# Transposes for attention and for the first branch: TensorE's, or VectorE's blocks by way of DRAM

## The chip, the cores and the metric

One core of a Trainium2 chip runs the kernel. The metric is the time of one execution on the device, in microseconds; each kernel is run several times and the median is given. Everything is float32.

## The reference

One layer of a hybrid network on 512 tokens of width 1024. It has two feed-forward halves and, between them, a mixing stage with two branches: a gated mLSTM and a forgetting attention of 16 heads of 64. All modulations (shift, scale, gate) come from one vector c through `w_ada`.

```python
u = rms_norm(x, ffn1_norm_g) * (1 + sc1) + sh1
x = x + 0.5 * g1 * swiglu(u, ffn1_w_in, ffn1_w_out)

u = rms_norm(x, mix_norm_g) * (1 + sc2) + sh2
z = u @ w_mix + b_mix            # q_m,k_m,v_m,o_m,i_m,f_m, q_f,k_f,v_f,f_f, g_a,g_b
h_m = mlstm_chunkwise(q_m, k_m, v_m, i_m, f_m)               # 4 heads, 128 / 256 wide
y_a = sigmoid(o_m) * rms_norm(h_m, mlstm_norm_g)             # first branch
y_b = forgetting_attention(q_f, k_f, v_f, f_f, fox_q_norm_g, fox_k_norm_g)  # 16 heads of 64
merged = sigmoid(g_a) * (y_a @ w_branch_a) + sigmoid(g_b) * (y_b @ w_branch_b)
x = x + g2 * (merged @ w_out)

u = rms_norm(x, ffn2_norm_g) * (1 + sc3) + sh3
x = x + 0.5 * g3 * swiglu(u, ffn2_w_in, ffn2_w_out)
```

## The kernel before

Every float32 product is made of three matmuls on split operands (`mm3`, lines 125 to 129): high by high, low by high, high by low. A weight comes from DRAM into one of three buffers `raw` (L92), ScalarE writes its high half `wh` (L102), VectorE its low half `wl` (L104), four buffers each. The same three `raw` buffers serve the rows of `w_ada`, which VectorE accumulates into `acc` (L302, L304); those are drawn in small steps (`self.ada`) wherever the program calls for one. All loads and stores named here are issued by SyncE (SP), in one queue.

The program is written as a dataflow: tiles come from pools with a fixed number of buffers, a scheduler orders the instructions of each engine, and waits follow from the tiles' reads and writes. So an edit in one place can change the order on every engine, near it and further away.

The mixing stage goes like this. `mlstm_h` (L1081) makes h of one mLSTM head in four blocks of 128 tokens (tile `hn`), scales each token's row (L1106, VectorE) and stores it to DRAM, `h_d` (L1107). `fox_qkv` (L1110) makes q and k of a group of four attention heads with tokens on the partitions (tiles `tk`, four of 128x512, normalized at L1138). `fox_t` (L1175) turns q and k of one pair of heads so that the 64 features of each head are on the partitions: TensorE transposes 128x128 blocks against an identity into PSUM (L1193), and ScalarE (L1198, L1202) and VectorE (L1200) split the result into high and low halves `fq`, `fk`, `klz`. `fox_s` (L1205) makes a head's scores and their softmax S, `fox_p` (L1235) transposes S (L1250) and splits it into `Ph` (L1248) and `Pl` (L1249), and `fox_o` (L1266) makes the output (L1280, then yt at L1283 and yb at L1284).

Between these steps, which wait much for each other, the main loop puts GEMM work: `advance(fill, n)` takes n steps of a generator. For the first twelve heads the filler is `fox_qkv` of the next group and then `gate` (one GEMM of 24 matmuls into PSUM tile g, a tanh at L1324, a store of `tg` to `g_d` at L1326); for the last four it is `y_a` (L1287) for m = 0 to 7. One `y_a` multiplies a 128-column slice of `w_mix` (w, 24 matmuls), takes the tanh `th` (L1300), loads a 128-column slice of h from DRAM (tile `ht`, L1302), transposes it on TensorE (L1305), scales it on ScalarE into `ya` (L1307), and multiplies with the gate (L1308). From m = 4 on each also draws two steps of `self.ada`. After it, two more gates and the branch's GEMMs follow, with `split_y` (L1343) in front of them.

The tiles `tk` and `ht` come from the same pool entry `"tok"` with four buffers. PSUM tiles come from `gbank` (GEMMs, g) and `tbank` (all else, t).

Of the kernel before, what the change touches and what calls it, by code (L numbers as in the profile page):

```python
# [11 lines left out]
F32 = mybir.dt.float32  # L12
F32R = mybir.dt.float32r
I32 = mybir.dt.int32
AF = mybir.ActivationFunctionType
# [5 lines left out]
P = 128  # L21
T = 512
NT = 4
D = 1024
NK = 8
# [19 lines left out]
MUL, ADD, SUB, MAX, MIN = ALU.mult, ALU.add, ALU.subtract, ALU.max, ALU.min  # L45


class Layer:
    def __init__(self, tc, es, A, out, dbg=None):
        self.tc, self.nc, self.es, self.A, self.out = tc, tc.nc, es, A, out  # L50
        self.dbg = dbg or {}
        pool = lambda name, **k: es.enter_context(tc.tile_pool(name=name, **k))
        self.cp = pool("const", bufs=1)
        self.up = pool("u", bufs=1)
        self.xp = pool("x", bufs=1)
        self.wp = pool("w", bufs=4)
        self.sp = pool("small", bufs=4)
        self.pg = pool("pg", bufs=4, space=PSUM)
        self.pt = pool("pt", bufs=4, space=PSUM)
        self.dp = pool("scr", bufs=1, space=DRAM)  # L60
        self.lo_after = None
        self.n = self.nx = self.now = 0
        self.due = []
        self.free = self.pin = lambda i: i

    def nm(self, s):
# [7 lines left out]
    def tick(self, n=1):  # L74
        for _ in range(n):
            self.now += 1
            for f in [f for t, f in self.due if t == self.now]:
                f()

    def tmp(self, pool, name):  # L80

# [999 lines left out]
    def mlstm_h(self, h, ip):  # L1081
        nc, sp = self.nc, self.sp
        (Wh, Wl), (vh, vl) = self.W[h], self.vt[h]
        ss = sp.tile([P, NT], F32, name=self.nm("hs"), tag="hs", bufs=2)
        hs = []
        for tb in range(NT):
            if tb % 2 == 0:
                h2 = ip.tile([P, 2, 256], F32, name=self.nm("hn"), tag="bc", bufs=4)
            ps = self.tbank()
# [12 lines left out]
        v = sp.tile([P, NT], F32, name=self.nm("hv"), tag="hv", bufs=2)  # L1102
        nc.vector.tensor_scalar(v, ss, 1.0 / 256, EPS, op0=MUL, op1=ADD)
        r = self.rsqrt(v, NT)
        for tb in range(NT):
            nc.vector.tensor_scalar(hs[tb], hs[tb], r[:, tb:tb + 1], None, op0=MUL)  # L1106
            nc.sync.dma_start(self.h_d[tb * P:(tb + 1) * P, h * 256:(h + 1) * 256], hs[tb])  # L1107


    def fox_qkv(self, g, ip):  # L1110

        nc, sp, w = self.nc, self.sp, self.A["w_mix"][0]
        o = g * 256
        bb = self.bias_bcast([(QF + o, 256), (KF + o, 256)], ip)
        tok = [ip.tile([P, 512], F32, name=self.nm("tk"), tag="tok", bufs=4) for _ in range(NT)]
# [20 lines left out]
        for tb in range(NT):  # L1136
            t3 = tok[tb].rearrange("p (h d) -> p h d", h=8)
            nc.vector.tensor_tensor(t3, t3, r[:, tb * 8:(tb + 1) * 8].unsqueeze(2).to_broadcast([P, 8, 64]), op=MUL)  # L1138
        if g == 3:
            self.fx[g] = tok, self.fx[g]  # L1140
            return
        gs = ((0,), (1,), (2, 3))[g]
        n = len(gs) * 256
# [12 lines left out]
        def mkv(ch):  # L1156
# [5 lines left out]
                wh, wl = self.split(r, sh)  # L1162
                return wh, wl, k * ch, k
            return make
        self.fx[g] = (tok, vts[0])
        if len(gs) > 1:
            self.fx[3] = vts[1]
# [7 lines left out]
    def fox_t(self, p, ap):  # L1175
# [11 lines left out]
        new = lambda n: ap.tile([P, T], F32R, name=self.nm(n), tag="qk", bufs=16)  # L1187
        q, k, kl = [new("fq") for _ in range(2)], [new("fk") for _ in range(2)], self.klz[p % 2]
        for i, R in ((0, R_FQ), (1, R_FK)):
            c = i * 256 + pr * P  # L1190
            b = self.tbank()
            for tb in range(NT):
                nc.tensor.transpose(b[:, tb * P:(tb + 1) * P], tok[tb][:, c:c + P], self.ident)  # L1193
            gc = self.colA[:, R + p:R + p + 1]
            for h in range(2):
                own, oth = lohi[h], lohi[1 - h]
                d = (q, k)[i][h]
                nc.scalar.activation(d[own, :], b[own, :], AF.Copy, scale=gc[own, :])  # L1198
                lo = q[h][oth, :] if i == 0 else kl[h][own, :]
                nc.vector.scalar_tensor_tensor(lo, b[own, :], gc[own, :], d[own, :], op0=MUL, op1=SUB)  # L1200
                if i:
                    nc.scalar.activation(k[h][oth, :], b[own, :], AF.Copy, scale=gc[own, :])  # L1202
# [81 lines left out]
        nc.vector.tensor_tensor(self.yb[2 * g + pr][rows, :], po[rows, :], tmp[rows, :], op=ADD)  # L1284


    def y_a(self, m, ap, ip):  # L1287
        nc = self.nc
        def step():
            if m >= NK // 2:  # L1290
                self.tick()
                next(self.ada)
        ps = self.gbank()
        w = self.w_stat(self.A["w_mix"][0], OM + m * P)
        self.gemm_stat(ps, w, 0, T, range(0, 4))
        step()
        yield
        self.gemm_stat(ps, w, 0, T, range(4, 8))
        th = self.tmp(ip, "th")
        nc.scalar.activation(th, ps, AF.Tanh, scale=0.5, bias=self.hom[:, m:m + 1])  # L1300
        ht = ip.tile([P, NT, P], F32, name=self.nm("ht"), tag="tok", bufs=4)
        nc.sync.dma_start(ht, self.h_d[:, m * P:(m + 1) * P].rearrange("(b p) n -> p b n", p=P))  # L1302
        b = self.tbank()
        for tb in range(NT):
            nc.tensor.transpose(b[:, tb * P:(tb + 1) * P], ht[:, tb, :], self.ident)  # L1305
        ya = ap.tile([P, T], F32, name=self.nm("ya"), tag="qk", bufs=16)
        nc.scalar.activation(ya, b, AF.Copy, scale=self.hmg[:, m:m + 1])  # L1307
# [46 lines left out]
    def run(self):  # L1354
# [2 lines left out]
        self.x_d = self.dp.tile([T, D], F32, name="x_d")  # L1357
        self.h_d = self.dp.tile([T, D], F32, name="h_d")
        self.v0_d = [self.dp.tile([P, 256], F32, name=f"v0_d{tb}") for tb in range(NT)]
        self.g_d = [self.dp.tile([P, T], F32, name=f"g_d{i}") for i in range(2 * NK)]  # L1360

        self.ntmp, self.xn_tiles, self.gb_tag = 4, self.xn_ffn, ("gb", 2)
# [144 lines left out]
        with tc.tile_pool(name="att", bufs=1) as ip:  # L1507
# [18 lines left out]
            def advance(gen, n):  # L1526
                for _ in range(n):
                    next(gen, None)
# [130 lines left out]
```

## Time and profile before

| | |
|---|---|
| median of 3 runs | 1320.24 us (1319.11 to 1320.57) |
| profiled execution, its own time | 1320.06 us |
| its span in the trace | 1318.2 us |
| TensorE clock granted | 1.000 |
| mLSTM heads and group 0 of q and k | 480 to about 550 us |
| attention loop | about 550 to 810 us |
| `y_a` GEMMs, m = 0 to 7 | about 753 to 819 us |

In the rows of the trace, PE is TensorE's matmuls, DVE VectorE, ACT ScalarE, SP SyncE. A row of the timeline has the start in us, the duration, the engine, the line of the kernel, the operation, output<-inputs by the program's names, and how many instructions are put together. A matmul's duration includes the pipeline's filling, so two matmuls of 0.39 us that start 0.23 us apart overlap; what one costs TensorE is read from the starts. The text in square brackets is the idle time ahead of an instruction and what ended it.

### The profile page before, as it was taken

Reading aid. Unit: us, or ns where it says so; the run is one execution under the profiler, and the core shown is the slowest. Engines: PE = TensorE matmul, PEld = TensorE weight load, DVE = VectorE, ACT = ScalarE, POOL = GpSimd, SP = SyncE. Lnnn points to the kernel's source line nnn. Section 1 sums busy time; section 2 is a strip of 40 time slices with the busy share of each in tenths; the row PEclk is TensorE's granted clock in tenths of the full one; section 3 lists DMA queues with packets and bytes.
Section 4 is the critical chain, followed back from the end, with each engine's and each line's share of the span. In section 5 each row is a group of like instructions: output and inputs, shape, how many; then the busy total and the mean of one; then the engine's idle time right before and its main releaser. Section 6 shows DMA issues by size and latency. Waiting matters only on the chain.

```text
span 1318.2 us, 17786 instructions
## 1 busy us (share of the span) xinstructions
PE 1303.2 (99%) x6341; PEld 1092.7 (83%) x6341; DVE 955.4 (72%) x1736; ACT 629.6 (48%) x1054; POOL 36.9 (3%) x57
## 2 busy tenths in 40 slices
PE   7999999999999999999999999999999999999998
PEld 6788888888899888888888888888898888888887
DVE  6887767478688687887887778777567556635787
ACT  5533232355476555566666666334372223223651
POOL 1000000000010101000000000003000000000000
PEclk9999999999999999999999999999999999999999
DMA  9899978465845334533342536777539777634574
GB/s 294 262 326 303 320 268 281 136 193 163 301 126 145 106 111 129 160 104 109 88 129 73 167 105 190 219 251 237 184 104 327 248 238 279 219 100 136 171 263 149
DMA packets 204488, 254.18 MB, mean 193 GB/s; under 512 B 15008, under 2 KB 146752, under 8 KB 204400
## 3 DMA queue, kind: packets, MB, share of 16 engines
q1 hardware_dynamic: 204016, 252.98, 60.4%
q8 instruction: 50, 0.82, 0.3%
q14 instruction: 38, 0.31, 0.1%
q0 software_dynamic: 320, 0.06, 0.0%
q10 hardware_dynamic: 64, 0.02, 0.0%
HBM read 217.28 MB, written 35.72 MB: 192 GB/s over the span
## 4 chain that ended last, share of the span: by engine, by line
PE 93%; DVE 3%; ACT 2%; DMA 1%; issue 1%; ACTq 0%; DVEq 0%
PE g L129 23%; PE g L127 23%; PE g L128 23%; PE t L127 4%; PE t L129 4%; PE t L128 4%; PE g L897 2%; PE t L1280 1%; PE t L1250 1%; PE t L1221 1%; PE t L897 1%; PE t L1222 1%; PE t L797 1%; ACT uh L263 0%; DVE wl L104 0%
## 5 line engine op out<-in xcount | busy, mean ns | idle before, releaser
L102 ACT ACTIVATE wh<-raw 128x1024 fp32r<-128x1024 f32 (+2 forms) x246 | 249.3, 1017 | 373.6 <-PE g L128 128.7
L104 DVE TENSOR_TENSOR wl<-raw,wh 128x1024 fp32r<-128x1024 f32 (+2 forms) x246 | 287.6, 1172 | 160.1 <-ACT wh L102 135.6
L127 PE MATMUL g<-uh,wh 128*128 128x512 f32 (+1 forms) x880 | 341.0, 388 | 0.0
L128 PE MATMUL g<-ul,wh 128*128 128x512 f32 (+1 forms) x880 | 339.5, 386 | 0.4 <-DVE ul L268 0.4
L129 PE MATMUL g<-uh,wl 128*128 128x512 f32 (+1 forms) x880 | 339.6, 386 | 0.0
L129 PEld LDWEIGHTS g<-uh,wl 128*128 128x128 f32 x880 | 165.3, 188 | 33.6
L128 PEld LDWEIGHTS g<-ul,wh 128*128 128x128 f32 x880 | 165.4, 188 | 33.0 <-DVE ul L268 0.6
L127 PEld LDWEIGHTS g<-uh,wh 128*128 128x128 f32 x880 | 165.3, 188 | 32.8 <-issue 0.6
L304 DVE SCALAR_TENSOR_TENSOR acc<-raw,ccol,acc 128x512 f32<-128x512 f32 (+1 forms) x70 | 66.7, 974 | 42.8 <-DMA raw<-in_w_ada_dram 42.7
L127 PE MATMUL g<-wh,uh 128*128 128x512 f32 (+1 forms) x256 | 97.5, 381 | 0.0
L129 PE MATMUL g<-wh,ul 128*128 128x512 f32 (+1 forms) x256 | 96.7, 378 | 0.0
L128 PE MATMUL g<-wl,uh 128*128 128x512 f32 (+1 forms) x256 | 96.4, 377 | 0.0
L127 PE MATMUL t<-wh,A 128*128 128x512 f32 x176 | 68.6, 390 | 0.0
L128 PE MATMUL t<-wl,A 128*128 128x512 f32 x176 | 68.5, 389 | 0.0
L129 PEld LDWEIGHTS g<-wh,ul 128*128 128x128 f32 x256 | 48.2, 188 | 9.0
L127 PEld LDWEIGHTS g<-wh,uh 128*128 128x128 f32 x256 | 48.2, 188 | 8.7 <-DVE tk L1118 0.5
L128 PEld LDWEIGHTS g<-wl,uh 128*128 128x128 f32 x256 | 48.2, 188 | 8.3
L129 PE MATMUL g<-yh,wl 128*128 128x512 f32 x128 | 50.0, 391 | 0.1
L127 PE MATMUL g<-yh,wh 128*128 128x512 f32 x128 | 49.8, 389 | 0.0
L128 PE MATMUL g<-yl,wh 128*128 128x512 f32 x128 | 49.8, 389 | 0.0
L420 ACT ACTIVATE A<-E 128x768 fp32r<-128x768 f32 x22 | 18.6, 846 | 53.4 <-DVE E L419 53.4
L1232 ACT ACTIVATE S<-S,mn 128x128 f32<-128x128 f32 (+1 forms) x64 | 35.5, 556 | 16.1 <-DVE mn L1224 9.9
(353 smaller groups left out, 2242.1 us busy)
## 6 DMA issues: line engine op xcount, KB each, us to landing
raw<-in_ffn_w_in_dram SPq DMA_DIRECT2D x82, 512.0 KB, 4.9
raw<-in_w_ada_dram SPq DMA_DIRECT2D x56, 512.0 KB, 5.7
raw<-in_w_mix_dram SPq DMA_DIRECT2D x46, 512.0 KB, 4.2
sa<-in_ffn_w_out_dram SPq DMA_DIRECT2D x22, 512.0 KB, 5.5
sb<-in_ffn_w_out_dram SPq DMA_DIRECT2D x44, 256.0 KB, 5.2
ws<-sa SPq DMA_DIRECT2D x22, 512.0 KB, 4.6
ws<-sb SPq DMA_DIRECT2D x44, 256.0 KB, 5.0
raw<-ws SPq DMA_DIRECT2D x44, 256.0 KB, 3.5
```

The costliest lines, as they stand in the source:

```text
L102: nc.scalar.activation(hi, src, AF.Copy)
L104: self.last_lo = nc.vector.tensor_tensor(lo, src, hi, op=SUB)
L127: pin(mm(ps, lh, rh, start=start, stop=False))
L128: pin(mm(ps, lh, rl, start=False, stop=False))
L129: self.last_mm = pin(mm(ps, ll, rh, start=False, stop=stop))
L304: nc.vector.scalar_tensor_tensor(a, r[:, s], c, a, op0=MUL, op1=ADD)
L420: nc.scalar.activation(A1[:, 0:3, :], E[:, 0:3, :], AF.Copy)
L797: pin(nc.tensor.transpose(cb[:, 384:512], self.ident, self.ident))
L897: pin(nc.tensor.matmul(acc_ps[b], (wl if p == 1 else wh)[:, b % 2, s], self.ul[k] if p == 2 else self.uh[k], start=k == 0 and p == 0, stop ...
L1221: nc.tensor.matmul(ps[:, :w], q[:, s], k[:, :w], start=True, stop=False)
L1222: nc.tensor.matmul(ps[:, :w], q[:, s], kl[:, :w], start=False, stop=True)
L1232: nc.scalar.activation(S[:, ws], S[:, ws], AF.Exp, scale=-1.0, bias=m, accum_out=sm[:, qb:qb + 1])
```

## The change

Three things are done in another way.

1. `mlstm_h`: the rows of h are scaled by ScalarE. Two blocks of 128 tokens by 256 make a tile of 128x512; VectorE transposes it in place in squares of 32x32, and one store instead of two takes it to `h_d`, one step of the filler later.
2. `fox_qkv` for groups 1 to 3: after L1138 VectorE transposes each `tk` tile in the same way, in place; it is stored to a new DRAM array `t_d[g]` one step later, and three steps later `bring` loads four tiles `fT` of 128x512 from it, in the order 0, 2, 1, 3 (q and k of the first pair of heads, then of the second). Each tile takes four loads (`blocks`) of 32 partitions by 16 squares by 32 elements, that is 512 runs of 128 bytes, so that the squares land transposed as a whole. `fox_t` then splits from `fT` in SBUF; group 0 stays with TensorE.
3. `y_a`: `ht` is loaded by `blocks` too, one m ahead (two at m = 0), and ScalarE scales it straight from SBUF. 

The delays are kept by a list `self.posts`, which `advance` counts down. In the new order of instructions the lines have other numbers: L1131 is a load of `blocks`, L1167 the store of `tk`, L105 the load of raw, L115 and L117 wh and wl, L1348 is th, L1350 ya, L1285 Ph, L1320 yt, L1369 the gate's store, L140 to L142 the three matmuls.

```diff
+    def post(self, steps, f):
+        self.posts.append([steps, f])
+
+    def advance(self, gen, n):
+        for _ in range(n):
+            next(gen, None)
+            for p in self.posts[:]:
+                p[0] -= 1
+                if p[0] < 0:
+                    self.posts.remove(p)
+                    p[1]()
...
         for tb in range(NT):
-            nc.vector.tensor_scalar(hs[tb], hs[tb], r[:, tb:tb + 1], None, op0=MUL)
-            nc.sync.dma_start(self.h_d[tb * P:(tb + 1) * P, h * 256:(h + 1) * 256], hs[tb])
+            nc.scalar.activation(hs[tb], hs[tb], AF.Copy, scale=r[:, tb:tb + 1])
+            if tb % 2:
+                t = h2s[tb // 2].rearrange("p b n -> p (b n)")
+                nc.vector.transpose(t, t)
+                self.post(1, lambda t=t, b=tb - 1: nc.sync.dma_start(
+                    self.h_d[b * P:(b + 2) * P, h * 256:(h + 1) * 256].rearrange("(b p) n -> p b n", p=P),
+                    t.rearrange("p (b n) -> p b n", b=2)))
+
+    def blocks(self, t, src):
+
+        for j in range(4):
+            self.nc.sync.dma_start(t[32 * j:32 * j + 32, :].rearrange("a (t b) -> a t b", b=32),
+                                   src[:, 32 * j:32 * j + 32].rearrange("(t a) b -> a t b", a=32))
...
             nc.vector.tensor_tensor(t3, t3, r[:, tb * 8:(tb + 1) * 8].unsqueeze(2).to_broadcast([P, 8, 64]), op=MUL)
+            if g:
+                t = tok[tb]
+                nc.vector.transpose(t, t)
+                self.post(1, lambda t=t, tb=tb: nc.sync.dma_start(self.t_d[g][tb * P:(tb + 1) * P, :], t))
+        def bring():
+            qk = [ip.tile([P, T], F32, name=self.nm("fT"), tag="tok", bufs=4) for _ in range(4)]
+            for n in (0, 2, 1, 3):
+                self.blocks(qk[n], self.t_d[g][:, n * P:(n + 1) * P])
+            self.fx[g][0] = qk
+        if g:
+            self.post(3, bring)
...
-            b = self.tbank()
-            for tb in range(NT):
-                nc.tensor.transpose(b[:, tb * P:(tb + 1) * P], tok[tb][:, c:c + P], self.ident)
+            if g:
+                b = tok[2 * i + pr]
+            else:
+                b = self.tbank()
+                c = i * 256 + pr * P
+                for tb in range(NT):
+                    nc.tensor.transpose(b[:, tb * P:(tb + 1) * P], tok[tb][:, c:c + P], self.ident)
...
+    def ht_load(self, m, ip):
+        t = ip.tile([P, T], F32, name=self.nm("ht"), tag="tok", bufs=4)
+        self.blocks(t, self.h_d[:, m * P:(m + 1) * P])
+        self.ht.append(t)
+
     def y_a(self, m, ap, ip):
...
         w = self.w_stat(self.A["w_mix"][0], OM + m * P)
+        if m == 0:
+            self.ht = []
+            self.ht_load(0, ip)
         self.gemm_stat(ps, w, 0, T, range(0, 4))
         step()
         yield
+        if m + 1 < NK:
+            self.ht_load(m + 1, ip)
         self.gemm_stat(ps, w, 0, T, range(4, 8))
+        ht = self.ht[m]
         th = self.tmp(ip, "th")
         nc.scalar.activation(th, ps, AF.Tanh, scale=0.5, bias=self.hom[:, m:m + 1])
-        ht = ip.tile([P, NT, P], F32, name=self.nm("ht"), tag="tok", bufs=4)
-        nc.sync.dma_start(ht, self.h_d[:, m * P:(m + 1) * P].rearrange("(b p) n -> p b n", p=P))
-        b = self.tbank()
-        for tb in range(NT):
-            nc.tensor.transpose(b[:, tb * P:(tb + 1) * P], ht[:, tb, :], self.ident)
         ya = ap.tile([P, T], F32, name=self.nm("ya"), tag="qk", bufs=16)
-        nc.scalar.activation(ya, b, AF.Copy, scale=self.hmg[:, m:m + 1])
+        nc.scalar.activation(ya, ht, AF.Copy, scale=self.hmg[:, m:m + 1])
```

Three places in the order of instructions follow; the numbers behind the names are the program's own, and they differ between the two kernels.

SyncE before, at the start of `y_a`: raw_7572, raw_7673 and raw_7756 are the weights of m = 2, 3 and 4.

```order
L92 DMA raw_7572<-in_w_mix_dram 128x8x128
L1326 DMA g_d_96<-tg_7150 128x512
L92 DMA raw_7673<-in_w_mix_dram 128x8x128
L1210 DMA A_1425_7505<-A_d 128x512
L1326 DMA g_d_97<-tg_7214 128x512
L92 DMA raw_7756<-in_w_mix_dram 128x8x128
L1326 DMA g_d_98<-tg_7260 128x512
L1302 DMA ht_7448<-h_d 128x4x128
```

SyncE now, at the same place: raw_7518, raw_7601 and raw_7700 are the weights of m = 1, 2 and 3, tg_7308 and tg_7398 those of the last two gates ahead of m = 0.

```order
L1369 DMA g_d_102<-tg_7308 128x512
L1131 DMA ht_7438<-h_d 32x16x32
L1369 DMA g_d_103<-tg_7398 128x512
L1131 DMA ht_7438<-h_d 32x16x32 x3
L1131 DMA ht_7467<-h_d 32x16x32 x4
L105 DMA raw_7518<-in_w_mix_dram 128x8x128
L1247 DMA A_1425_7536<-A_d 128x512
L1131 DMA ht_7566<-h_d 32x16x32 x4
L105 DMA raw_7601<-in_w_mix_dram 128x8x128
L1131 DMA ht_7647<-h_d 32x16x32 x4
```

Before, the weights of m = 2 to 4 stood ahead of the first load of h; now the weight of m = 1 stands behind the last gate's store and behind the eight loads of the first two tiles of h, and each later weight behind four more.

ScalarE before, around the last three `y_a`: th_7913 and th_8004 are the tanh of m = 5 and 6, wh_8035 is the high half for m = 7, wh_8108 for the gate behind it.

```order
L102 ACTIVATE wh_8035<-raw_8033 128x1024
L1300 ACTIVATE th_7913<-g_7850,hom 128x512
L1307 ACTIVATE ya_7922<-t_7917,hmg 128x512
L1283 ACTIVATE yt_7938<-t_7929 64x512
L1248 ACTIVATE Ph_7969<-t_7973 128x512
L1248 ACTIVATE Ph_7969<-t_7980 128x512
L1248 ACTIVATE Ph_7969<-t_7987 128x256
L102 ACTIVATE wh_8108<-raw_8106 128x1024
L319 ACTIVATE fo_8139<-acc_7774 64x512
L319 ACTIVATE fo_8139<-acc_7775 64x512
L1300 ACTIVATE th_8004<-g_7941,hom 128x512
```

ScalarE now, at the same place: th_7941 and th_8030 are the tanh of m = 5 and 6, wh_7965 and wh_8054 the high halves for m = 6 and 7.

```order
L1348 ACTIVATE th_7941<-g_7873,hom 128x512
L1320 ACTIVATE yt_7959<-t_7950 64x512
L1285 ACTIVATE Ph_7990<-t_8008 128x256
L1350 ACTIVATE ya_8032<-ht_7924,hmg 128x512
L115 ACTIVATE wh_7965<-raw_7963 128x1024
L1348 ACTIVATE th_8030<-g_7962,hom 128x512
L1320 ACTIVATE yt_8048<-t_8039 64x512
L1350 ACTIVATE ya_8088<-ht_8013,hmg 128x512
L115 ACTIVATE wh_8054<-raw_8052 128x1024
```

The high half for m = 7 stood ahead of the tanh of m = 5; now it stands behind the tanh of m = 6.

TensorE before, from the end of the GEMM of m = 6 (g_7941) to the start of that of m = 7 (g_8032):

```order
L129 MATMUL g_7941<-uh_3271,wl_7945 128x512
L1305 MATMUL t_8008<-ident,ht_8006 128x128 x4
L1280 MATMUL t_8020<-Ph_7969,fvt_6266 128x512
L1280 MATMUL t_8020<-Pl_7970,fvt_6266 128x512
L1280 MATMUL t_8020<-Ph_7969,fvt_6266 128x384
L1280 MATMUL t_8020<-Pl_7970,fvt_6266 128x384
L1280 MATMUL t_8020<-Ph_7969,fvt_6266 128x256
L1280 MATMUL t_8020<-Pl_7970,fvt_6266 128x256
L1280 MATMUL t_8020<-Ph_7969,fvt_6266 128x256
L1280 MATMUL t_8020<-Pl_7970,fvt_6266 128x256
L127 MATMUL g_8032<-uh_3264,wh_8035 128x512
```

TensorE now, at the same place (g_7962 is m = 6, g_8051 m = 7):

```order
L140 MATMUL g_7962<-uh_3275,wh_7965 128x512
L141 MATMUL g_7962<-ul_3283,wh_7965 128x512
L142 MATMUL g_7962<-uh_3275,wl_7966 128x512
L140 MATMUL g_8051<-uh_3268,wh_8054 128x512
L141 MATMUL g_8051<-ul_3276,wh_8054 128x512
L142 MATMUL g_8051<-uh_3268,wl_8055 128x512
```

The transposes of `ht` are gone, and the output of the last head stands ahead of the GEMM of m = 6 instead of behind it, so the two GEMMs follow each other directly.

More of the change, by code (lines that the diff above doesn't have):

```diff
@@ L63, in __init__ @@
         self.due = []
+        self.posts = []
         self.free = self.pin = lambda i: i
@@ L1084, in mlstm_h @@
         ss = sp.tile([P, NT], F32, name=self.nm("hs"), tag="hs", bufs=2)
-        hs = []
+        hs, h2s = [], []
         for tb in range(NT):
@@ L1088, in mlstm_h @@
                 h2 = ip.tile([P, 2, 256], F32, name=self.nm("hn"), tag="bc", bufs=4)
+                h2s.append(h2)
             ps = self.tbank()
@@ L1138, in fox_qkv @@
             nc.vector.tensor_tensor(t3, t3, r[:, tb * 8:(tb + 1) * 8].unsqueeze(2).to_broadcast([P, 8, 64]), op=MUL)
+            if g:
[9 more added lines that the diff above has]
+            self.post(3, bring)
         if g == 3:
-            self.fx[g] = tok, self.fx[g]
             return
@@ L1164, in mkv @@
             return make
-        self.fx[g] = (tok, vts[0])
-        if len(gs) > 1:
-            self.fx[3] = vts[1]
+        for i, vt in zip(gs, vts):
+            self.fx[i] = [tok, vt]
         if g:
@@ L1189, in fox_t @@
         for i, R in ((0, R_FQ), (1, R_FK)):
-            c = i * 256 + pr * P
-            b = self.tbank()
-            for tb in range(NT):
-                nc.tensor.transpose(b[:, tb * P:(tb + 1) * P], tok[tb][:, c:c + P], self.ident)
+            if g:
[5 more added lines that the diff above has]
+                    nc.tensor.transpose(b[:, tb * P:(tb + 1) * P], tok[tb][:, c:c + P], self.ident)
             gc = self.colA[:, R + p:R + p + 1]
@@ L1359, in run @@
         self.v0_d = [self.dp.tile([P, 256], F32, name=f"v0_d{tb}") for tb in range(NT)]
+        self.t_d = [self.dp.tile([T, 512], F32, name=f"t_d{g}") for g in range(4)]
         self.g_d = [self.dp.tile([P, T], F32, name=f"g_d{i}") for i in range(2 * NK)]
@@ L1525, in run @@
             self.vt, self.W, self.fx, self.qkt, self.S = [None] * 4, {}, {}, {}, {}
-            def advance(gen, n):
-                for _ in range(n):
-                    next(gen, None)
+            advance = self.advance
             advance(self.v_mlstm(0, ip, ip), 99)
```

## The prediction

> **What bounds the kernel now.** I began with the page: its busy times, and the chain that ended last.
>
> ```profile
> span 1318.2 us, 17786 instructions
> PE 1303.2 (99%) x6341; PEld 1092.7 (83%) x6341; DVE 955.4 (72%) x1736; ACT 629.6 (48%) x1054; POOL 36.9 (3%) x57
> PE 93%; DVE 3%; ACT 2%; DMA 1%; issue 1%; ACTq 0%; DVEq 0%
> ```
>
> TensorE is busy 99% of the span and makes up 93% of the chain. Whatever leaves TensorE shortens the program and whatever makes TensorE wait lengthens it; work of the other engines counts only through such waits. Next I read the busy times by window over the end of the stage that is changed, and TensorE's waits from 480 to 850 us.
>
> ```profile
> core 0: us, PE busy (x) PEld busy (x) DVE busy (x) ACT busy (x) POOL busy (x), PEclk, DMA share, GB/s
> 700.00:750.00 50.00, 49.70 (x252) 41.09 (x251) 37.88 (x91) 30.22 (x58) 0.00 (x0) 1.00 0.44 122
> 750.00:800.00 50.00, 49.57 (x265) 41.44 (x264) 40.18 (x115) 35.19 (x80) 0.00 (x0) 1.00 0.40 124
> 800.00:850.00 50.00, 50.00 (x242) 41.62 (x241) 40.01 (x58) 23.79 (x37) 0.00 (x0) 1.00 0.67 204
> ```
>
> ```profile
> PE t L1250 <- DVE fq L1200: 0.5, 2, 0.3
> PE t L127 <- DVE fq L1200: 0.4, 1, 0.4
> PE t L1250 <- ACT fk L1202: 0.3, 1, 0.3
> ```
>
> TensorE idles 0.8 us of these 150, VectorE is at some 80% and ScalarE between 48 and 70%. The three largest waits in 370 us sum to 1.2 us, and all three are for the splits that follow the transposes of q and k. So there is nothing to win but the transposes and these 1.2 us, and everything to lose: 50.00 of 50.00 us busy from 800 to 850 us means that the weights for each GEMM lay ready there.
>
> **What leaves TensorE.** All 64 transposes of L1193 but the 16 of head pairs 0 and 1 go, and all 32 of L1305: 48 + 32 = 80.
>
> ```profile
> L1193 PE MATMUL t<-ident,tk x64: 270/272/273, 534.9 to 745.2; 128*128 128x128 f32 x64
> L1305 PE MATMUL t<-ident,ht x32: 270/272/273, 761.6 to 819.4; 128*128 128x128 f32 x32
> 743.33 0.39 PE L129 MATMUL g<-uh,wl 128*128 128x512 f32 x1
> 743.56 1.91 PE L1193 MATMUL t<-ident,tk 128*128 128x128 f32 x16
> 745.22 0.48 PE L127 MATMUL g<-uh,wh 128*128 128x512 f32 x1
> 745.54 0.39 PE L128 MATMUL g<-ul,wh 128*128 128x512 f32 x1
> ```
>
> The 272 ns of one are not its price, since matmuls are pipelined: the timeline's starts are. Sixteen take 745.22 − 743.56 = 1.66 us, and the step from the matmul behind them to its successor is 0.32 us (745.54 − 745.22) where 0.23 is usual (743.56 − 743.33), 0.09 more; so 1.75/16 = 0.109 us each, and 80 × 0.109 = 8.7 us. Of the 1.2 us of waits I take 1.0 as gone, because the splits' source now lies ready. Gain: **9.7 us**.
>
> **VectorE and ScalarE.** Added to VectorE are 20 transposes of 128x512 (8 for h, 12 for q and k); the 16 scalings of h move to ScalarE.
>
> ```profile
> L1106 DVE TENSOR_SCALAR hn<-hn,rq x16: 344/347/1386, 488.6 to 548.1; 128x256 f32<-128x256 f32 x16
> L1242 DVE TENSOR_SCALAR S<-S,sm 128x512 f32<-128x512 f32 x4 | 1.9, 479 | 0.0
> L1138 DVE TENSOR_TENSOR tk<-tk,rq x16: 680/683/691, 530.4 to 725.2; 128x512 f32<-128x512 f32 x16
> L104 DVE TENSOR_TENSOR wl<-raw,wh 128x1024 fp32r<-128x1024 f32 x9 | 11.0, 1222 | 4.8 <-ACT wh L102 2.7 <-PE t L1193 2.1
> ```
>
> The trace shows no transpose on VectorE. Bounds are 0.479 us (the cheapest operation of that size) and 1.222 us (twice the size); I take 0.683, the row in the same place and shape. That is 20 × 0.683 = 13.7 us against 16 × 0.347 = 5.6 us that go, 8 us net over some 240 us, on an engine with a fifth of its time free. The four transposes of a group stand in the same burst as L1138, and add 4 × 0.683 = 2.7 us to it; what is behind them on VectorE are the weights' low halves, cut well ahead there. I cost this at nothing; without that cover it would be up to 2.7 us for each of three groups. [...] The scalings on ScalarE, 16 of some 0.4 us over 70 us, are hidden by its idle time.
>
> **The way through DRAM.** For each of groups 1 to 3 the path from L1138 to the first split becomes store, landing, 16 block loads, landing.
>
> ```profile
> L1138 DVE TENSOR_TENSOR tk<-tk,rq x2: 681/682/682, 588.4 to 589.0; 128x512 f32<-128x512 f32 x2
> L1198 ACT ACTIVATE fq<-t,colA x1: 682/682/682, 604.7 to 604.7; 64x512 fp32r<-64x512 f32 x1
> 745.60 2.09 SPq L1302 DMA_DIRECT2D ht<-h_d  x4
> DMA to landing us min/median/max: 2.8/2.8/2.8
> ```
>
> Group 1 has the least room: 604.7 − (589.0 + 0.7) = 15.0 us. It needs a last transpose (0.7), a store of 256 KB (2.8 at the price of ht's load), eight loads for the first head pair at 2.09/4 = 0.52 us an issue (4.2) and a landing (2.8): 10.5 us. It fits, with 4.5 us to spare. A further 2.8 us to the second pair's tiles is not needed at once. But each train also holds SyncE's queue for 16 × 0.52 = 8.4 us, and each ht for 4 × 0.52 = 2.1 where it held it 0.5. What stands behind them on SyncE are the weights.
>
> **What makes TensorE wait.** Before, the weights of the first-branch GEMMs run far ahead:
>
> ```profile
> 739.12 0.38 SPq L92 DMA_DIRECT2D raw<-in_w_mix_dram  x1
> ...
> 767.41 0.38 SPq L92 DMA_DIRECT2D raw<-in_w_mix_dram  x1
> raw<-in_w_mix_dram SPq DMA_DIRECT2D x46, 512.0 KB, 4.2
> ```
>
> The row at 739.12 us is the fifth of the eight, 22 us before the transposes that follow the first GEMM (L1305's first start, 761.6); the sixth follows at 767.41. In the changed order (SyncE's rows in the section on the change) the second, raw_7518, stands behind the stores of all the gates and behind eight block loads, and each later one behind four more. From then on the lead is gone: the ring of three raw buffers goes weight, ada, ada, weight, so each weight waits until its predecessor has been split. ScalarE's order shows what that means: wh_8054, the last weight's high half, stands behind th_8030, the tanh of the GEMM before it, and TensorE's rows have no work between these two GEMMs. Before, wh_8035 stood ahead of the tanh of the GEMM two earlier. The prices:
>
> ```profile
> L102 ACT ACTIVATE wh<-raw 128x1024 fp32r<-128x1024 f32 x10 | 10.6, 1060 | 8.7 <-DMA raw<-in_w_mix_dram 4.8 <-DMA raw<-in_w_branch_a_dram 2.1 <-PE g L128 1.7
> L1300 ACT ACTIVATE th<-g,hom 128x512 f32<-128x512 f32 x8 | 5.5, 684 | 4.9 <-PE g L129 4.9
> L1307 ACT ACTIVATE ya<-t,hmg 128x512 f32<-128x512 f32 x8 | 5.4, 680 | 0.0
> L1283 ACT ACTIVATE yt<-t 64x512 f32<-64x512 f32 x7 | 4.1, 591 | 0.1
> L1248 ACT ACTIVATE Ph<-t 128x512 fp32r<-128x512 f32 x12 | 6.6, 596 | 5.2 <-PE t L1250 5.2
> L1248 ACT ACTIVATE Ph<-t 128x256 fp32r<-128x256 f32 x6 | 2.4, 392 | 0.0
> 758.55 0.47 PE L1280 MATMUL t<-Ph,fvt 128*128 128x512 f32 x1
> ...
> 759.92 0.40 PE L129 MATMUL g<-uh,wl 128*128 128x512 f32 x1
> ...
> 761.99 1.25 PE L1250 MATMUL t<-ident,S 128*128 128x128 f32 x10
> 763.00 0.48 PE L127 MATMUL g<-uh,wh 128*128 128x512 f32 x1
> 819.05 0.60 PE L1305 MATMUL t<-ident,ht 128*128 128x128 f32 x4
> 819.30 0.69 ACT L1300 ACTIVATE th<-g,hom 128x512 f32<-128x512 f32 x1 [0.93 <-PE g L129]
> ```
>
> A tanh starts 0.25 us (819.30 − 819.05) after TensorE's next work. Ten transposes of S take 1.0 us (763.00 − 761.99), the eight matmuls of an output (fox_o) 1.4 (759.92 − 758.55), and I put the eight of a head's scores (fox_s) at the same.
>
> - Last GEMM (m = 7): 0.25 + tanh 0.68 + yt 0.59 + ya 0.68 + wh 1.06 = 3.3 us until the high half is there. Two matmuls (0.46) run on it, the third needs the low half, 1.22 later: 0.8 more. **4.0 us.**
> - m = 6: the same with one more Ph of 0.39, 3.65 + 0.8 = 4.4, less two transposes of S and an output in between (1.6). **2.8 us.**
> - m = 5: yt waits for an output (1.4 after the GEMM, + 0.25), then yt 0.59, Ph 0.6 + 0.6 + 0.39, ya 0.68, two small copies of 0.31 and wh 1.06: 6.2 us, less 3.4 us of outputs and transposes in between; the low half is covered by more of these. **2.5 us**, some of it overlapped.
> - m = 1: raw_7518 goes out some 8.5 us after the last gate's GEMM (its tanh behind other ScalarE work, about 4.8, then store and seven block loads at 0.5), + 4.2 landing + 1.06 + 1.22 − 0.46 = 14.5, where TensorE arrives after 10.7 (two scores, an output, ten transposes, one GEMM of 24 × 0.23). **4.0 us**; ScalarE's queue alone (tanh, three Ph, two ya, wh against 2.4 us of other TensorE work) gives 3.
> - The gate behind m = 7 gets its raw buffer only when m = 7's weight is split: 0.4 + 4.2 + 1.06 + 1.22 − 0.46 = 6.4 against a GEMM of 5.5, and a wake-up or two: **1.3 us.**
> - m = 2 and 3, whose first two matmuls stand apart in the new order: 0.5 each, **1.0**; and in group 2 a weight of the next group that now stands behind a gate's store: **1.2** (0 to 1.5).
>
> Sum: 4.0 + 2.8 + 2.5 + 4.0 + 1.3 + 1.0 + 1.2 = **16.8 us** lost against 9.7 won: +7.1. On the profiled execution's 1320.06 us that is 1327.2; it lies 0.2 us below the median of the runs, so I say **1327.4 us**. Counting only what the order of instructions forces (4.0, 2.8, 1.5, 3.0, 0.5) the loss is 11.8 and the time 1322; with every small-block term at its upper end (6 us more) it is 1333.
>
> **The rivals.**
>
> *The gain mostly stays.* If the weights land earlier than I work out, so that only the two last GEMMs wait, the loss is 4.0 + 2.8, and the time 1320.1 − 9.7 + 6.8 = 1317.2; with no wait at all 1310.4. For it: ScalarE idles a third of the time and the DMA engines more than half from 700 to 800 us. Against it: wh_8054 behind th_8030 is a matter of order, not of speed. 0.20, most of it between 1313 and 1317.
>
> *The block loads are slow.* A load of a 32x512 block row moves 512 runs of 128 B, the loads before 512 of 512 B.
>
> ```profile
> q1 hardware_dynamic: 204016, 252.98, 60.4%
> ```
>
> This row has packets, MB and the share of 16 engines. A packet, 1240 B on average, costs 0.604 × 16 × 1318.2 / 204016 = 0.062 us of one engine. If a 128 B run cost as much, one block load would take 512 × 0.062 / 16 = 2.0 us and a group's eight 16 instead of 4.2: 12 us more, where the room is 4.5. That is 7.5 us in group 1 and some 3 to 4 in groups 2 and 3, whose room is some 4 us larger; with the seven loads ahead of raw_7518 10 us more. Together up to 25 us: 1352. It decides from about 0.9 us a load. [...] No row here shows runs of 128 B. 0.12.
>
> *The change doesn't do what it says*: TensorE's new order has no transpose left in head pairs 2 to 7 or in the first branch, so I give this nothing.
>
> **How the numbers follow.** About 0.2%, 2.6 us, can be told from no change here. My own case (1321 to 1334) has 0.64, of which 0.04 lies within 0.2%; the gain that stays 0.20, of which 0.02 is within; slow loads 0.12; 0.04 for worse that I don't see. So faster 0.18, same 0.06, slower 0.76. The range, 1315 to 1338, leaves out the best of the first rival and most of the second.
>
> **What would show it.** Right: no L1193 or L1305 rows after 600 us; TensorE waits of 2.5 to 4 us ahead of the GEMMs m = 1, 5, 6 and 7, put down to wh (ScalarE) or wl (VectorE); TensorE's busy sum about 9 us lower; block loads landing in under 3 us. Wrong: these GEMMs start without a gap (then it is faster), or fq of groups 1 to 3 waits for the block loads (then it is much slower than I say).

## The result

| | median | ratio to the kernel before, 95% interval |
|---|---|---|
| before, 5 runs | 1319.71 us | |
| after, 5 runs | 1331.56 us (1331.02 to 1332.5) | 1.0089 [1.0078, 1.01] |

The change costs 11.8 us; the forecast was 7.1. The span of the profiled execution grew from 1318.2 to 1329.1 us, by 10.9. The lines of the page of the changed kernel that answer to those shown of before:

```profile
span 1329.1 us, 17780 instructions
PE 1301.7 (98%) x6261; PEld 1089.2 (82%) x6261; DVE 960.5 (72%) x1740; ACT 637.7 (48%) x1070; POOL 37.0 (3%) x57
PE 86%; DVE 5%; DMA 3%; ACT 3%; issue 1%; SPq 1%; POOL 0%; ACTq 0%; DVEq 0%; POOLq 0%
DMA packets 244105, 260.48 MB, mean 196 GB/s; under 512 B 57184, under 2 KB 184832, under 8 KB 244016
```

TensorE runs 80 matmuls fewer, but is busy only 1.5 us less, while its share of the chain fell from 93 to 86%. Where the time went is seen in the windows (the window, its length, then the busy time of TensorE, weight loads, VectorE, ScalarE, GpSimd, with the number of instructions; granted clock, share of the DMA engines, GB/s) and in TensorE's waits from 480 to 850 us:

```profile
700.00:750.00 50.00, 50.00 (x250) 42.31 (x249) 39.56 (x105) 31.52 (x65) 0.00 (x0) 1.00 0.39 97
750.00:800.00 50.00, 43.79 (x210) 35.20 (x209) 33.27 (x94) 30.00 (x70) 0.00 (x0) 0.93 0.66 141
800.00:850.00 50.00, 43.95 (x177) 34.67 (x177) 34.80 (x50) 20.43 (x31) 0.00 (x0) 0.90 0.65 190
```

```profile
PE g L140 <- ACT wh L115: 6.3, 3, 3.1
PE g L142 <- DVE wl L117: 1.8, 2, 1.2
PE t L1317 <- DVE Pl L1286: 1.7, 2, 1.6
PE t L1317 <- ACT Ph L1285: 0.8, 1, 0.8
PE t L1317 <- DVE yb L1321: 0.7, 1, 0.7
```

Until 750 us next to nothing is lost. In the 100 us of the first branch TensorE idles 12.3 us, where it had idled 0.4: 8.1 us for the halves of weights (the first two rows), the rest for tiles of the attention's softmax and output (Pl, Ph, yb). And the granted clock is below 1.00, which it was nowhere in this stretch in the kernel before. One such place, ahead of the GEMM of m = 7, in TensorE's timeline:

```profile
817.90 0.39 PE L142 MATMUL g<-uh,wl 128*128 128x512 f32 x1
821.38 0.74 PE L140 MATMUL g<-uh,wh 128*128 128x512 f32 x1 [3.08 <-ACT wh L115]
821.92 0.63 PE L141 MATMUL g<-ul,wh 128*128 128x512 f32 x1
823.11 0.79 PE L142 MATMUL g<-uh,wl 128*128 128x512 f32 x1 [0.56 <-DVE wl L117]
823.70 0.63 PE L140 MATMUL g<-uh,wh 128*128 128x512 f32 x1
824.12 0.63 PE L141 MATMUL g<-ul,wh 128*128 128x512 f32 x1
```

Two losses stand here one behind the other. First the wait for wh, 3.08 us, and for wl, 0.56. Then matmuls that start 0.42 us apart (823.70 to 824.12) where 0.23 is usual: half the clock, and 0.50 is what was granted from 826 to 828 us. The same happens twice more, and the windows of 5 us (columns as above) show how long it lasts:

```profile
760.00:765.00 5.00, 3.77 (x9) 2.50 (x9) 4.02 (x17) 2.58 (x9) 0.00 (x0) 0.50 1.05 190
765.00:770.00 5.00, 5.00 (x19) 3.96 (x19) 1.41 (x5) 0.92 (x2) 0.00 (x0) 0.81 1.06 198
810.00:815.00 5.00, 4.56 (x14) 3.43 (x15) 2.84 (x5) 0.00 (x0) 0.00 (x0) 0.66 0.66 190
820.00:825.00 5.00, 3.06 (x7) 1.96 (x8) 4.34 (x6) 1.32 (x2) 0.00 (x0) 0.65 0.36 116
825.00:830.00 5.00, 5.00 (x17) 3.96 (x16) 2.19 (x3) 1.84 (x3) 0.00 (x0) 0.67 0.99 294
```

Weighted with TensorE's busy time, which is an estimate, the clock took 3.77 × 0.50 + 5 × 0.19 + 4.56 × 0.34 + 3.06 × 0.35 + 5 × 0.33 = 7.1 us. TensorE's busy time bears it out: 8.7 less for the transposes and 7.1 more for the clock make 1.6 less, and 1.5 is measured. So: 8.7 won, 12 to 13 lost in waits, 7 in the clock, which sums to 10 to 11 and is what the span shows.

### The profile page after: what moved, and what is told of

It reads as the page before. It is cut to its first block, busy times and chain, and to the rows that moved or that the text cites. A ratio compares the mean times of both kernels' runs of the same rounds, so it can differ in the third digit from the quotient of the medians.

```text
span 1329.1 us, 17780 instructions
## 1 busy us (share of the span) xinstructions
PE 1301.7 (98%) x6261; PEld 1089.2 (82%) x6261; DVE 960.5 (72%) x1740; ACT 637.7 (48%) x1070; POOL 37.0 (3%) x57
## 4 chain that ended last, share of the span: by engine, by line
PE 86%; DVE 5%; DMA 3%; ACT 3%; issue 1%; SPq 1%; POOL 0%; ACTq 0%; DVEq 0%; POOLq 0%
PE g L142 22%; PE g L141 22%; PE g L140 22%; PE t L140 4%; PE t L142 4%; PE t L141 4%; PE g L910 1%; PE t L1317 1%; PE t L1287 1%; DMA raw<-in_w_ada_dram 1%; DVE wl L117 1%; PE t L1258 1%; PE t L1259 1%; PE t L910 1%; SPq L821 1%
## 5 line engine op out<-in xcount | busy, mean ns | idle before, releaser
L115 ACT ACTIVATE wh<-raw 128x1024 fp32r<-128x1024 f32 (+2 forms) x246 | 249.1, 1016 | 368.2 <-PE g L141 125.6
L117 DVE TENSOR_TENSOR wl<-raw,wh 128x1024 fp32r<-128x1024 f32 (+2 forms) x246 | 287.7, 1172 | 152.6 <-ACT wh L115 132.1
L140 PE MATMUL g<-uh,wh 128*128 128x512 f32 (+1 forms) x880 | 343.3, 390 | 6.4 <-ACT wh L115 6.3
L142 PE MATMUL g<-uh,wl 128*128 128x512 f32 (+1 forms) x880 | 342.7, 389 | 1.8 <-DVE wl L117 1.8
L140 PEld LDWEIGHTS g<-uh,wh 128*128 128x128 f32 x880 | 167.0, 190 | 41.1 <-ACT wh L115 7.7
L142 PEld LDWEIGHTS g<-uh,wl 128*128 128x128 f32 x880 | 166.9, 190 | 38.0 <-DVE wl L117 3.9
L140 PE MATMUL g<-wh,uh 128*128 128x512 f32 (+1 forms) x256 | 96.6, 379 | 0.0
L142 PE MATMUL g<-wh,ul 128*128 128x512 f32 (+1 forms) x256 | 96.5, 377 | 0.0
L140 PE MATMUL t<-wh,A 128*128 128x512 f32 x176 | 68.6, 390 | 0.0
L142 PEld LDWEIGHTS g<-wh,ul 128*128 128x128 f32 x256 | 48.2, 188 | 9.1
L140 PEld LDWEIGHTS g<-wh,uh 128*128 128x128 f32 x256 | 48.1, 188 | 8.4
L142 PE MATMUL g<-yh,wl 128*128 128x512 f32 x128 | 50.0, 391 | 0.2 <-DVE wl L117 0.2
L140 PE MATMUL g<-yh,wh 128*128 128x512 f32 x128 | 49.8, 389 | 0.0
```

Of the source, the lines that this page charges most:

```text
L115: nc.scalar.activation(hi, src, AF.Copy)
L117: self.last_lo = nc.vector.tensor_tensor(lo, src, hi, op=SUB)
L140: pin(mm(ps, lh, rh, start=start, stop=False))
L142: self.last_mm = pin(mm(ps, ll, rh, start=False, stop=stop))
```

## The experiments

Theory A: the weights come late, by their place in SyncE's queue and, behind that, in ScalarE's order. Theory B: the small loads themselves are slow or fill the DMA engines. Ratios are to the kernel before, run on the same chip beside each.

### One part alone

The first run keeps the change for q and k and takes `mlstm_h` and `y_a` from before; the second keeps those two and takes `fox_qkv` and `fox_t` from before.

> Only q and k of groups 1 to 3 go by VectorE and DRAM; h is scaled, stored, loaded and transposed as before. 48 transposes of 0.109 us leave TensorE (5.2 us) and about 1 us of waits. Theory A (the order of SyncE's queue: the weights of the first branch come late because they stand behind group 3's block loads and the gates' stores): the loads stay, so the weights stay late, though with two block loads fewer per GEMM ahead of them; some 4 to 10 us of waits remain, the time is 1318 to 1324 us. Theory B (the eight small loads of h in front of the first weights, and their traffic, do it): without them nothing waits, 1313 to 1315 us.

> Only h goes by VectorE's blocks and small loads; q and k are transposed by TensorE as before. 32 transposes of 0.109 us leave TensorE (3.5 us). Theory A: SyncE's rows have the weights of m = 1 to 4 ahead of the loads of h again, as before, so hardly a GEMM waits: 1316 to 1318 us. Theory B: the small loads still fill the DMA engines and hold the queue from m = 5 on, several microseconds of waits: 1322 us or more.

Measured: q and k alone 0.997 [0.9958, 0.9982], 1316.15 us; h alone 1.0041 [1.0027, 1.0055], 1325.57 us. Against 1320.05 us these are −3.9 and +5.5: together +1.6, where the whole change has +11.8. So the two parts also hurt each other. The first time is between the numbers of the two theories, below A's. The second is B's number, and TensorE waits where B has it, from m = 5 on: 0.85 us at m = 5, 0.46 + 1.05 + 0.58 at m = 6, 2.13 + 1.61 at m = 7. But the last and longest of these isn't made by slow loads. ScalarE's timeline of the kernel with h alone, at the GEMM of m = 7, and its weight's issue on SyncE:

```profile
808.34 0.40 SPq L105 DMA_DIRECT2D raw<-in_w_mix_dram  x1
```

```profile
813.69 0.69 ACT L1336 ACTIVATE th<-g,hom 128x512 f32<-128x512 f32 x1 [6.81 <-PE g L142]
814.40 0.59 ACT L1308 ACTIVATE yt<-t 64x512 f32<-64x512 f32 x1
815.02 1.06 ACT L115 ACTIVATE wh<-raw 128x1024 fp32r<-128x1024 f32 x1
```

A weight of this stage lands 3.9 us after its issue (median), so at about 812.2. ScalarE was idle for 6.81 us until 813.69, but wh stands behind a tanh that needs TensorE's result. That wait is one of order. At m = 5 and 6 it is the same: these weights were asked for at 771.47 and 796.66 us and split at 793.67 and 805.20, each behind a tanh. The wait ahead of m = 1 and the clock's fall at 760 us are in neither kernel alone; they come from the two parts together.

### The gates' stores on another queue

```diff
-            nc.sync.dma_start(self.g_d[8 * i + m], th)
+            nc.gpsimd.dma_start(self.g_d[8 * i + m], th)
```

> The changed kernel, with the gates' stores (g_d) posted by GpSimd's queue instead of SyncE's; all else as it was. Theory A: SyncE no longer sits on the stores of four gates that wait for their tanh (from 728 to 750 us in the trace of the changed kernel), the weight of m = 1 goes out some 6 to 10 us earlier, and most waits of the first branch go, with the fall of the clock behind them: 1312 to 1319 us. Theory B (slow or colliding small loads): the loads of h are all still there ahead of the weights, and the time stays above 1326 us.

Measured: 1.0036 [1.0023, 1.0049], 1324.85 us, 7 us better than the change, and between the two theories' numbers. In the changed kernel SyncE's timeline shows what the weight of m = 1 stood behind:

```profile
720.41 7.92 SPq L1131 DMA_DIRECT2D fT<-t_d  x15
728.43 11.43 SPq L1369 DMA_DIRECT2D g_d<-tg  x3
739.95 0.38 SPq L1131 DMA_DIRECT2D ht<-h_d  x1
749.67 0.32 SPq L1369 DMA_DIRECT2D g_d<-tg  x1
750.03 3.79 SPq L1131 DMA_DIRECT2D ht<-h_d  x7
753.87 0.49 SPq L105 DMA_DIRECT2D raw<-in_w_mix_dram  x1
```

From 728 to 750 us SyncE waits for the tanh of one gate after another, with h and the weight queued behind. With the stores elsewhere the weight of m = 1 goes out at 735.66 us, 18 us earlier. 0.78 and 0.53 us are left of the wait of 2.55 + 1.23 + 0.66 ahead of m = 1, and the clock stays at 1.00 there. The 3 us ahead of m = 7 stay as they were, which is right for A's second half: that wait isn't made by SyncE's stores.

### Filling the waits

```diff
+        n = {1: 12, 7: 12}.get(m, 0)
+        if n:
+            b = self.tbank()
+            with self.tc.issue_after(self.last_ya.ins):
+                for i in range(n):
+                    nc.tensor.matmul(b, self.uh[0][:, 0:P], self.ul[0], start=i == 0, stop=i == n - 1)
         self.gemm_stat(ps, w, 0, T, range(0, 4))
...
         self.gemm_stat(ps, w, 0, T, range(4, 8))
+        self.last_ya = self.last_mm
```

> The changed kernel, with 12 more matmuls of 128x512 in TensorE's two longest waits (ahead of the GEMMs of m = 1 and m = 7); their result is not used. They take 2.8 us each and change nothing in what is waited for. If the lower clock behind a wait costs time by itself (0.43 instead of 0.23 us a matmul in some 14 and 17 matmuls), the kernel gets faster by 3 to 7 us with more work in it: 1325 to 1328 us. If the waits alone are the cost, the time stays at 1331 to 1333 us, or grows.

Measured: 1.0084 [1.0067, 1.01], 1330.49 us; not to be told from the change (1.0089). The clock did what was expected, and its gain was lost again further on. With the extra matmuls the windows 760 to 765 and 820 to 825 us have a clock of 1.00, and the GEMM of m = 7 starts at 818.32 us instead of 821.38. Its last matmul starts at 824.97 us instead of 830.42, 5.4 us earlier, so up to there the clock's fall in these two places had cost time by itself. But then the gate behind it waits:

```profile
815.07 2.88 PE L1345 MATMUL t<-ul,uh 128*128 128x512 f32 x12
818.32 0.50 PE L140 MATMUL g<-uh,wh 128*128 128x512 f32 x1 [0.37 <-ACT wh L115]
...
826.57 0.50 PE L140 MATMUL g<-uh,wh 128*128 128x512 f32 x1 [1.20 <-ACT wh L115]
827.83 0.57 PE L142 MATMUL g<-uh,wl 128*128 128x512 f32 x1 [0.53 <-DVE wl L117]
```

A GEMM at half the clock had been long enough to hide the next weight; at full clock it isn't, and 1.7 us of wait come back, with a fall of the clock behind them (0.81 from 825 to 830 us, 0.85 from 830 to 835). The branch's first GEMM starts at 840.01 us instead of 841.53: 1.5 us are left of the 5.4. So the clock's 7 us and the waits' 12 are not simply added: a faster GEMM gives part of it back as long as the weights arrive just in time. What the clock would cost the whole program if the weights came earlier stays open.

### The loads of h on another queue; weights asked for earlier

The fifth run posts the loads of `ht` from GpSimd's queue (`blocks` now takes the queue as a third argument); the sixth asks for each weight two GEMMs ahead.

```diff
-        self.blocks(t, self.h_d[:, m * P:(m + 1) * P])
+        self.blocks(t, self.h_d[:, m * P:(m + 1) * P], self.nc.gpsimd)
```

```diff
-        w = self.w_stat(self.A["w_mix"][0], OM + m * P)
         if m == 0:
-            self.ht = []
+            self.ht, self.wa = [], []
+        while len(self.wa) < min(m + 3, NK):
+            self.wa.append(self.w_stat(self.A["w_mix"][0], OM + len(self.wa) * P))
+        w = self.wa[m]
+        if m == 0:
             self.ht_load(0, ip)
```

> The changed kernel, with the small loads of h posted by GpSimd's queue; the loads of q and k stay on SyncE. All weights of the first branch then stand free of them on SyncE, and in ScalarE's new order wh of m = 7 stands ahead of the tanh of m = 5 again, as it did before the change. Theory A (the place of the weights in the queue and in ScalarE's order): the waits at m = 5, 6 and 7 go, the clock stays up, 1311 to 1315 us, faster than both kernels. Theory B (runs of 128 B are slow or fill the DMA engines): the loads are the same ones, TensorE waits for ya or for the weights as before, 1320 us or more. If GpSimd takes more than 2 us to post one, h comes late and it is theory B's number for another reason, to be seen in the landing times.

> The changed kernel, with each first-branch weight asked for two GEMMs ahead (three at m = 0). On SyncE the weights of m = 1 to 7 stand earlier by one to two groups of small loads; but in ScalarE's order wh of m = 7 still stands behind the tanh of m = 6. If the order on ScalarE is what makes m = 7 wait, that wait of 3 to 4 us stays, only that ahead of m = 1 goes: 1323 to 1328 us. If the landing of the weight makes it wait, both go: 1313 to 1318 us.

Measured: h's loads on GpSimd 0.9961 [0.9948, 0.9973], 1317.51 us beside 1322.09 for the kernel before; that is faster than before, by 4.6 us, and between the two theories' numbers, nearer to A's. The waits ahead of m = 5, 6 and 7 are gone; the clock is 1.00 from 765 to 850 us. The same loads, 128 B at a time, landing in 4.5 us in the median, cost these three GEMMs nothing once no weight stands behind them, and theory B falls for them. What is left are waits of 0.76 and 0.87 us for Pl, one of 1.05 for mn, and one of 2.07 for wl in the GEMM of m = 1, at 758 us. This one begins with a transfer, since wl stands on VectorE behind this row:

```profile
756.19 0.69 DVE L1250 TENSOR_TENSOR Am<-A,maskF 128x512 f32<-128x512 f32 x1 [2.11 <-DMA A<-A_d]
```

A was asked for at 751.04 us. The DMA engines are full there: their share is 1.14 and 1.17 from 755 to 765 us, at 225 and 220 GB/s. In the first run, where h comes in larger pieces, it is 1.14 and 1.12, but at 316 and 327 GB/s. So B keeps a part at m = 1: with the small loads the engines are as busy with some 30% fewer bytes. What that costs no run separates.

Weights two ahead: 1.004 [1.0028, 1.0051], 1327.37 us beside the same 1322.09. The time is A's, but only in part for the reason given. The waits of the weights ahead of m = 1 are gone. Ahead of m = 7 1.94 us stay, and ScalarE's timeline shows that they are of order; the weight's issue on SyncE stands first:

```profile
790.06 0.40 SPq L105 DMA_DIRECT2D raw<-in_w_mix_dram  x1
```

```profile
801.50 0.59 ACT L1320 ACTIVATE yt<-t 64x512 f32<-64x512 f32 x1 [0.62 <-PE t L1317]
802.12 0.69 ACT L1351 ACTIVATE th<-g,hom 128x512 f32<-128x512 f32 x1
802.71 1.05 ACT L115 ACTIVATE wh<-raw 128x1024 fp32r<-128x1024 f32 x1
```

Asked for at 790.06, this weight had 12 us to land and was still split only behind the tanh. The larger loss is new. The next weight, the gate's, now stands behind three loads of `w_ada` and is asked for at 816.14 us, and TensorE waits 9.6 us for it:

```profile
PE g L140 <- ACT wh L115: 11.6, 2, 9.6
```

### The versions that are faster, and a control

> Only q and k by VectorE and DRAM (as in the first run of this study) and the gates' stores on GpSimd's queue. In that run TensorE still waits 2.5 us ahead of m = 1 and 1.3 us once more, since the weight of m = 1 stands behind gate stores. Theory A: with these gone from SyncE the waits go and the time is 1312 to 1314 us. Rival: the waits have to do with VectorE's order, they stay, 1316 us.

> The changed kernel with both the small loads of h and the gates' stores on GpSimd's queue. Theory A (place of the weights): the wait of 2.2 us ahead of m = 1 that was left with the loads of h alone moved goes too; all 80 transposes are gone and nothing waits: 8 to 10 us below the kernel before (ratio 0.992 to 0.994). Rival: GpSimd's queue (0.65 us a load, in order, behind stores that wait for a tanh) now brings h late, and it is no better than 0.996.

> The kernel before with the gates' stores on GpSimd's queue, nothing else. It has no such wait to lose, since its weights run ahead of the stores: same as the kernel before within 0.2%. If it gets faster by 3 us, the gain of moving the stores in the other runs is none of the change's.

Measured: q and k alone with the gates' stores on GpSimd 0.9937 [0.9918, 0.9956], 1313.43 us; the whole change with both h's loads and the gates' stores there 0.9936 [0.992, 0.9953], 1312.91 us; the kernel before with the stores there 1.0016 [1.0007, 1.0026]. So the stores' queue alone brings nothing to the kernel before, and both versions beat both kernels by 8 us and more. The first run's wait isn't ahead of m = 1, as I had put it: TensorE waits 2.30 us within a head's scores, until 774 us, for mn on VectorE, which stands behind the low half of a weight that landed late (ScalarE had waited 3.01 us for it). With the stores elsewhere it is gone, as A has it. The first version has 48 transposes less (5.2 us) and its largest wait from 480 to 900 us is this:

```profile
PE g L142 <- DVE wl L117: 0.9, 1, 0.9
```

The second has 80 less and isn't faster, because a weight lands late (asked for at 761.50 us, split at 769.73, with ScalarE idle for 5.92 us before that; 4.2 from issue to landing is the median before), which makes wl late, Pl stands behind wl on VectorE, and TensorE idles 3.56 us and then runs at half the clock (matmuls of 128x512 0.43 us apart from 774.23 to 778.50 us):

```profile
768.99 0.28 PE L1259 MATMUL t<-klz,fq 128*128 128x256 f32 x1
772.82 0.58 PE L1258 MATMUL t<-fk,fq 128*128 128x256 f32 x1 [3.56 <-DVE Pl L1286]
```

### VectorE's transposes: thrice, and none

```diff
                 nc.vector.transpose(t, t)
+                nc.vector.transpose(t, t)
+                nc.vector.transpose(t, t)
                 self.post(1, lambda t=t, tb=tb: nc.sync.dma_start(self.t_d[g][tb * P:(tb + 1) * P, :], t))
```

The run without any leaves this line out (on the version with the gates' stores on GpSimd), so its squares stay as they are and its output is another.

> Only q and k by VectorE and DRAM, with each of the 12 transposes on VectorE done three times (in place, which gives the same tile): 24 more of 0.68 us, 16 us of work on VectorE. If VectorE's transposes lie off the path that sets the end, as the forecast has it, the time is that of the first run of this study within 1.5 us, 1315 to 1318 us. If they are on it, 5.5 us a group: 1325 us or more.

> Only q and k by DRAM, gates' stores on GpSimd's queue, and without the 12 transposes on VectorE, which leaves the squares untransposed (the output is another one). It prices one transpose per tile, where three cost 17 us more than one. If VectorE's cover is used up only beyond one (the forecast: nothing), it is as fast as the same kernel with them, ratio 0.993 to 0.995; if each transposition costs its 0.68 us, it is 8 us faster, ratio 0.987.

Measured: thrice 1.0102 [1.0082, 1.0122]; none 0.995 [0.9935, 0.9965]. None is no faster than one (0.9937): the 12 transposes of the change lie beside other work. But 24 more cost 0.0132 × 1320 = 17 us, all of their 16.5 us, so I was wrong to expect the cover to reach that far. Some 4 us of it are the clock's, worked out as above (0.67 and 0.64 from 680 to 690 us, 0.66 from 790 to 795). TensorE's longest waits in that run, 560 to 850 us, are for what VectorE has queued behind the transposes, and for one weight that landed late (the last row; ScalarE waited 1.20 us for it):

```profile
PE t L1255 <- DVE Pl L1283: 3.8, 4, 1.5
PE g L141 <- DVE wl L117: 3.8, 2, 3.3
PE g L140 <- ACT wh L115: 2.7, 1, 2.7
```

The cover of a group ends somewhere between 2.7 us (one transpose per tile) and 8.2 (three).

## Why the prediction was right, and where it was off

- **What leaves TensorE.** 80 transposes went. Of the 1.2 us of waits, of which I took 1.0 as gone, 0.7 is still there: 0.32 (now for hn) and 0.18 with group 0, and 0.20 for a split of group 1. So some 9.2 us were won, not 9.7.
- **VectorE and ScalarE.** The transposes take 0.69 and 0.70 us, nearly what the row of the same shape had (0.683), and cost nothing, as forecast (none against one). The scalings take 0.496 us on ScalarE, not 0.4, and no wait in TensorE's list names them.

```profile
L1166 DVE STREAM_TRANSPOSE tk<-tk x12: 667/688/709, 588.0 to 715.6; 128x512 f32<-128x512 f32 x12
L1123 DVE STREAM_TRANSPOSE hn<-hn x8: 665/704/711, 489.5 to 548.7; 128x512 f32<-128x512 f32 x8
L1120 ACT ACTIVATE hn<-hn,rq x16: 492/496/510, 488.3 to 548.2; 128x256 f32<-128x256 f32 x16
```

- **The way through DRAM.** It fits: the first split of group 1 starts at 599.44 us, 5 us earlier than before, and the 16 loads of a train are issued 0.53 us apart (7.92/15). They land in 2.4 us (2.2 to 3.0), no slower than 256 KB did (2.8), and a load is 64.0 KB. The rival of slow loads is gone with that for q and k. For h it isn't quite: these loads land in 4.2 us in the median, not in under 3, where the 256 KB took 2.8, and the weights between them in 5.5 where I took 4.2.
- **What makes TensorE wait.** The places were right, and at m = 1 and m = 7 the mechanism too: the weights behind the stores and block loads on SyncE, and behind the tanh on ScalarE. By place, forecast and measured: m = 1 4.0 and 4.4 (0.66 + 2.55 + 1.23); m = 5 2.5 and 1.6; m = 6 2.8 and 2.4; m = 7 4.0 and 3.6; the gate behind it 1.3 and 0, since m = 7 at half the clock hid it (1.7 when it ran at full clock); m = 2, 3 and group 2 2.2 and 0.6. In sum 16.8 and 12.6. At m = 6 I had the wrong operand. TensorE waits there for the last head's output, which stands ahead of this GEMM, and then finds wh ready and wl just in time:

```profile
808.47 0.39 PE L1317 MATMUL t<-Ph,fvt 128*128 128x256 f32 x1 [0.83 <-ACT Ph L1285]
810.44 0.39 PE L1317 MATMUL t<-Pl,fvt 128*128 128x256 f32 x1 [1.58 <-DVE Pl L1286]
810.90 0.39 PE L140 MATMUL g<-uh,wh 128*128 128x512 f32 x1
```

```profile
807.42 0.69 DVE L1351 SCALAR_TENSOR_TENSOR ya<-th,ya 128x512 f32<-128x512 f32 x1 [3.64 <-ACT th L1348]
809.97 0.41 DVE L1286 TENSOR_TENSOR Pl<-t,Ph 128x256 fp32r<-128x256 f32 x1
```

Pl stands on VectorE behind ya, which waits for the tanh of m = 5, and behind yb and two accumulations of `w_ada`: an order behind the tanh again, but on the other engine and for another tile. The weight's wh came at 809.97 us (808.92 + 1.05), too late as well, only hidden. Of the 1.6 us at m = 5, too, only 0.70 are for wh; 0.74 are for yb and 0.16 for Pl.

- **The step that failed in size** is the sum's missing term: the clock. I took 0.23 us for every matmul behind a wait, and 0.43 was true of some 35 of them, 7 us. The terms of waiting were too high by 4, the missing one too low by 7, and the forecast came out 4.7 us short. That it isn't further off is partly luck, since these two errors go against each other.
- **The gain that mostly stays** had its condition right (only order, not speed, keeps wh back) and is what the fifth run shows when the order is freed: there the split for m = 7 stands ahead of the tanh of m = 5 again (797.79 and 802.21 us).

I had also named the ring of three raw buffers as what ends the lead. The sixth run shows that it is only part of it: asking earlier moved the wait from m = 1 to the gate. Why the order of ScalarE puts wh behind the tanh when small loads share SyncE's queue, and ahead of it when they don't, is decided when the program is scheduled; that it reckons these loads as slower than they are would fit, but no run here shows it.

## What to carry to other kernels

When work leaves the engine that bounds the program by way of extra transfers, price the queue position of everything that is issued behind them, and read the new order on the engine that prepares the next operand: an operand that is prepared behind a result of the GEMM before it makes the bounding engine wait, however early it lands: in the sixth run such a weight had 12 us to land, and TensorE waited 1.94. Put such transfers on a queue that carries nothing the bounding engine needs: here the 80 transposes then bring 8 us instead of costing 12, and 48 of them bring as much. And reckon that a wait on TensorE of two or three microseconds can cost more than its length: here some 35 matmuls behind three such places took 0.43 us instead of 0.23, 7 us in sum.

## What was not expected of the hardware

TensorE's granted clock fell from 1.00 to 0.50 behind short waits. In the changed kernel it was down after 2.55 us of idling (756.78 to 759.72 us), after 0.83 + 1.58 us with one matmul in between, and after 3.08 us; it stayed down for some 3 to 7 us (811.1 to 814.7 us the shortest, 759.7 to 766.8 the longest), with matmuls of 128x512 0.43 us apart. That the idling makes it fall, the fourth run shows: with the waits at m = 1 and 7 filled, the clock is 1.00 there, and at m = 6, which was left as it was, it falls again (0.76 from 805 to 810 us). A wait of 2.07 us was followed by it in the fifth run (0.76 from 760 to 765 us). One of 2.30 us in the first run was not (its clock is 1.00 in all windows), nor was one of 3.30 us in the run with three transposes (1.00 from 640 to 660 us), so length alone doesn't decide. What else does, no run here shows.
